# Two chained transformer blocks on one core: attention products gathered into runs, and the recurrence's output products split by shape

## The chip, the cores and the metric

The kernel runs on 1 core of one Trainium2 chip. The metric is the device time of one execution in microseconds, the median of several runs. Engines are called PE (TensorE, matmul), PEld (its weight loads), DVE (VectorE), ACT (ScalarE), POOL (GpSimd) and SP (SyncE, which issues most DMAs). Every time below is in us unless marked ns.

## The reference

512 tokens and 256 context tokens of width 1024 pass through two chained blocks. The first has two layers, an even one (latent attention beside a convolution) and an odd one (a recurrence in two directions beside a neighbourhood attention), each followed by 16 experts; the second has a forgetting attention and a sparse attention, each followed by a convolution FFN. What the change touches, cut short:

```python
def dense_attention(q, k, v):                      # even layer, 8 heads, q/k 96, v 64
    s = jnp.einsum('bqhd,bkhd->bhqk', q, k).astype(jnp.float32) * scale
    return jnp.einsum('bhqk,bkhd->bqhd', jax.nn.softmax(s, -1), v)
# tokens: keys and values of tokens and context (768); context: of the context alone (256)

def wkv7_step(S, inp):                             # odd layer, 8 heads of 64, both directions
    r, w, k, v, a, b = inp
    sa = jnp.einsum('bhvk,bhk->bhv', S, a)
    S = S * w[:, :, None, :] + sa[..., None] * b[:, :, None, :] + v[..., None] * k[:, :, None, :]
    return S, jnp.einsum('bhvk,bhk->bhv', S, r)

# forgetting attention, 16 heads of 64, causal, 512 tokens
s = jnp.einsum('bhqd,bhkd->bhqk', qb, k) * scale + cb[..., :, None] - c[..., None, :]
p = jax.nn.softmax(jnp.where(causal, s, -jnp.inf), axis=-1)
o = jnp.einsum('bhqk,bhkd->bqhd', p, v)

# sparse attention, 16 heads in 2 key groups: compressed, selected and window parts, gated
o = g[:, :, 0] * o_c + g[:, :, 1] * o_s + g[:, :, 2] * o_w
```

## The kernel before

`body` (line 2871) runs the stages one behind the other: `even_stage`, `moe`, `odd_stage`, `moe`, `fa_stage`, `conv_ffn`, `ns_stage`, `conv_ffn`. A scheduler that simulates the engines sets the order of instructions on each engine, except inside `attend` (line 575), which fixes the order on PE and ACT by hand.

**The attentions.** `attend` gives each group of heads two passes. The first pass computes scores with queries on the partitions to find a normaliser per query (its log-sum, turned into the tile `LT`). The second pass computes scores again with keys on the partitions, adds the normaliser as one more matmul (line 542, `S.add`), takes an exponential on ACT into a tile `PT`, and multiplies `PT` with the values. A step of the loop at line 595 issues, in this order: a piece of side work, the first pass's scores of this step, the exponential of the second pass's last step (`b1`), the products of the step before that (`b2`), the second pass's scores of this step, the first pass's exponentials. So the products of a tile stand two steps behind its scores.

- Even attention (`even_attend`, line 1472): `second` walks over the pairs of heads, in a pair over its two heads, in a head over seven key tiles of 128: tiles 0 to 5 for the 512 tokens' queries, and step 6 with the context's queries against the two context tiles. Each step makes one score bank (line 1488, three split products for each), one exponential of 128 × 512 and one product (line 1502; line 1505 in step 6, two of 256 columns). The product's output has 64 rows, so one head fills one half (`HALF`) of a bank's partitions. `PT` has 4 buffers, score banks (`tb`) 2, output banks 2. The conv of the even layer runs on DVE, POOL and ACT beside the first stretch of it.
- Forgetting attention (`fa_attend`, line 779): `second` walks over pairs of heads and four key tiles; a step has both heads of a pair: two score banks, two exponentials (line 805), two products (line 813), which write the two halves of one bank. Tile j has 512 − 128 j columns. `PT` has 6 buffers.
- Sparse attention (`ns_attend`, line 1166): the same with two branches b (selected and window); scores at lines 1186 to 1188, exponential at 1195, products at 1203.

**The recurrence.** `odd_stage` (line 2665) runs `rec_steps` (line 2499) for the context (b = 0) and the two halves of the tokens (b = 1, 2), four chunks of 64 tokens each. `chunk(s)` prepares what doesn't depend on the state; `scan(s)` carries the state S: x = A·S (line 2567, 64 × 64 tiles, 16 matmuls), added on DVE (line 2568); Z·x (line 2572), copied to `UV`; the new state from `UV` and `BT` (line 2580); and for b > 0 the output y: for each of 16 units (8 pairs of head and direction by two heads) S·R (line 2592, 64 × 64 tiles) and `UV`·`AMr` (line 2593, 128 × 64) into the same 64 × 64 piece of one bank, then an add on DVE (line 2600). There are 8 scan steps with y. Banks of the recurrence (`rb`) number 5 (`ODD_BANKS`). Beside it the scheduler weaves the neighbourhood attention (`odd_attend`), the output product of the odd layer (`odd_out`, line 2361) and `ada_steps` (line 1624), which computes the second layer's modulation from 24 loads `aw` of 512 KB through one buffer (line 1644).

## Time and profile before

| | us |
|---|---|
| median of 3 runs | 4043.91 |
| lowest to highest | 4041.24 to 4044.95 |
| the profiled execution | 4059.11 |
| its span | 4057.0 |
| its mean granted TensorE clock | 0.944 |

Where the edited code lies in the span of the profiled execution: even attention, second passes from 366 to 527; the outputs y of the recurrence from 1775 to 2042; products of the forgetting attention from 2790 to 2887; of the sparse attention from 3471 to 3652.

How to read it: the span is one execution from its first instruction to its last. An engine's busy time counts its instructions, not its waits. The granted clock is the share of full speed that PE was given (1.00 is 2.4 GHz, 0.50 is 1.2 GHz). In a timeline neighbouring instructions of the same kind are one entry, with their count behind "x"; starts of successive entries tell how long PE was held, since the end of one overlaps the start of the next. A matmul of fp32 operands counts as two passes in the even and later attentions' products and in the recurrence (so 16 matmuls are x32).

### The profile page before, as it was taken

Reading aid. Unit: us, or ns where it says so; the run is one execution under the profiler, and the core shown is the slowest. Engines: PE = TensorE matmul, PEld = TensorE weight load, DVE = VectorE, ACT = ScalarE, POOL = GpSimd, SP = SyncE. Lnnn points to the kernel's source line nnn. Section 1 sums busy time; section 2 is a strip of 40 time slices with the busy share of each in tenths; the row PEclk is TensorE's granted clock in tenths of the full one; section 3 lists DMA queues with packets and bytes.
Section 4 is the critical chain, followed back from the end, with each engine's and each line's share of the span. In section 5 each row is a group of like instructions: output and inputs, shape, how many; then the busy total and the mean of one; then the engine's idle time right before and its main releaser. Section 6 shows DMA issues by size and latency. Waiting matters only on the chain.

```text
span 4057.0 us, 53307 instructions
## 1 busy us (share of the span) xinstructions
PE 3757.1 (93%) x21365; PEld 2531.7 (62%) x21365; DVE 2090.8 (52%) x3363; ACT 1591.7 (39%) x2687; POOL 493.0 (12%) x603
## 2 busy tenths in 40 slices
PE   7999997999998989798979988899999998999999
PEld 4666474656565778676643332376688876557887
DVE  4747337777777564635252222464355556425544
ACT  3446424555554622431121000257433335643332
POOL 1542011000002122313010000220000012100000
PEclk8998998999998999788879999999999999999999
DMA  7430027888883461214279999622223231003231
GB/s 238 150 117 16 16 103 293 345 317 349 311 338 140 165 189 58 63 33 143 70 282 398 407 411 418 245 89 89 83 95 97 89 95 46 1 27 104 94 99 68
DMA packets 264344, 678.69 MB, mean 167 GB/s; under 512 B 16048, under 2 KB 142016, under 8 KB 214816
## 3 DMA queue, kind: packets, MB, share of 16 engines
q1 hardware_dynamic: 256832, 653.48, 43.9%
q0 software_dynamic: 7264, 21.80, 1.7%
q8 instruction: 168, 2.75, 0.3%
q14 instruction: 80, 0.66, 0.0%
HBM read 641.86 MB, written 32.83 MB: 166 GB/s over the span
## 4 chain that ended last, share of the span: by engine, by line
PE 39%; DMA 12%; DVE 2%; ACT 1%; issue 1%; POOL 0%; SPq 0%; POOLq 0%; ACTq 0%; DVEq 0%
PE bk L374 26%; DMA mw<-in_moe_w_dram 9%; DMA aw<-in_ada_w_dram 1%; PE bk L1992 1%; PE ob L1203 1%; PE rb L2593 1%; PE rb L2592 1%; PE tb L1186 1%; PE bk L1644 1%; PE tb L542 1%; DMA w<-in_a_w_in_dram 1%; PE tb L1187 0%; PE ob L813 0%; PE ob L374 0%; PE bk L2361 0%
## 5 line engine op out<-in xcount | busy, mean ns | idle before, releaser
L351 DVE TENSOR_TENSOR wl<-w,wh 128x1024 fp32r<-128x1024 f32 (+2 forms) x157 | 256.4, 1637 | 280.2 <-ACT wh L350 279.7
L350 ACT CAST wh<-w 128x1024 fp32r<-128x1024 f32 (+2 forms) x157 | 215.6, 1375 | 393.9 <-PE bk L374 341.0
L351 DVE TENSOR_TENSOR wpl<-mw,wph 128x1024 fp32r<-128x1024 f32 x256 | 302.1, 1221 | 31.5 <-ACT wph L350 22.7
L374 PE MATMUL bk<-xTh,wh 128*128 128x512 f32 x704 | 275.7, 393 | 6.9 <-DVE xTl L354 6.9
L350 ACT CAST wph<-mw 128x1024 fp32r<-128x1024 f32 x256 | 258.3, 1047 | 48.7 <-PE bk L1919 30.5
L374 PE MATMUL bk<-xTl,wh 128*128 128x512 f32 x704 | 275.3, 391 | 0.0
L374 PE MATMUL bk<-xTh,wl 128*128 128x512 f32 x704 | 275.3, 391 | 0.0
L1992 PE MATMUL bk<-mw,xgT 128*64 128x512 f32 x1024 | 239.5, 604 | 24.4 <-DMA mw<-in_moe_w_dram 23.5
L2028 PE MATMUL bk<-mw,hidT 128*64 128x512 f32 x1024 | 250.1, 615 | 1.2 <-ACT hidT L2020 0.7
L1992 PEld LDWEIGHTS bk<-mw,xgT 128*64 128x64 f32 x1024 | 70.3, 138 | 177.0 <-issue 129.3
L1919 PE MATMUL bk<-wph,xgPh 128*96 128x512 f32 x512 | 162.3, 397 | 1.3 <-ACT xgPh L1896 1.3
L1919 PE MATMUL bk<-wph,xgPl 128*96 128x512 f32 x512 | 160.2, 394 | 0.0
L1919 PE MATMUL bk<-wpl,xgPh 128*96 128x512 f32 x512 | 158.3, 394 | 0.0
L2028 PEld LDWEIGHTS bk<-mw,hidT 128*64 128x64 f32 x1024 | 72.5, 140 | 136.0 <-issue 126.7
L374 PEld LDWEIGHTS bk<-xTh,wh 128*128 128x128 f32 x704 | 133.4, 190 | 35.2 <-DVE xTl L354 7.3
L374 PEld LDWEIGHTS bk<-xTl,wh 128*128 128x128 f32 x704 | 133.3, 189 | 27.5
L374 PEld LDWEIGHTS bk<-xTh,wl 128*128 128x128 f32 x704 | 133.0, 189 | 27.9
L1877 POOL DMA_INDIRECT xg<-moe_xn,IDX x32 | 31.9, 997 | 878.9 <-PE tb L1889 852.9
L374 PE MATMUL bk<-wh,gTh 128*128 128x512 f32 x352 | 136.9, 389 | 0.0
L374 PE MATMUL bk<-wl,gTh 128*128 128x512 f32 x352 | 136.9, 389 | 0.0
L374 PE MATMUL bk<-wh,gTl 128*128 128x512 f32 x352 | 136.9, 389 | 0.0
L253 POOL TENSOR_TENSOR hr<-hr,mhalf 128x4 f32<-128x4 f32 (+3 forms) x77 | 91.6, 1197 | 262.3 <-DVE hr L485 256.8
(771 smaller groups left out, 8402.4 us busy)
## 6 DMA issues: line engine op xcount, KB each, us to landing
mw<-in_moe_w_dram SPq DMA_DIRECT2D x384, 1024.0 KB, 11.1
aw<-in_ada_w_dram SPq DMA_DIRECT2D x96, 512.0 KB, 4.3
w<-in_f_w_up_dram SPq DMA_DIRECT2D x40, 1024.0 KB, 5.1
w<-in_f_w_down_dram SPq DMA_DIRECT2D x16, 1024.0 KB, 4.9
w<-in_a_w_in_dram SPq DMA_DIRECT2D x24, 512.0 KB, 3.5
w<-in_od_w_in_dram SPq DMA_DIRECT2D x15, 512.0 KB, 4.5
w<-in_ev_w_in_dram SPq DMA_DIRECT2D x12, 512.0 KB, 4.8
rw_bk<-bk SPq DMA_DIRECT2D x8, 768.0 KB, 4.2
```

Source lines behind the costliest of these rows:

```text
L253: return self.nc.gpsimd.tensor_tensor(t, t, self.mhalf[:p].to_broadcast([p, n]), op=ALU.pow)
L350: nc.scalar.copy(h, src)
L351: nc.vector.tensor_sub(l, src, h.bitcast(F32))
L374: self.nc.tensor.matmul(out, lhsT=L[a], rhs=R[b], start=start and n == 0, stop=stop and n == len(pairs) - 1)
L542: self.k.nc.tensor.matmul(s, lhsT=self.k.selb[0:self.nr, h:h + 1].to_broadcast([self.nr, 128]), rhs=LT, start=False, stop=stop)
L1186: nc.tensor.matmul(s[:, q0:], lhsT=KA[:, b, kv, sl], rhs=QA[:, h, q0:], start=True, stop=False)
L1203: nc.tensor.matmul(o[HALF[u], q0:], lhsT=V[j][:, b, kv * 64:(kv + 1) * 64], rhs=PT[u][:, q0:], start=b == 0 and j == 0, stop=False)
L1644: nc.tensor.matmul(ps[32 * g:32 * g + 32, :], lhsT=k.silc[:, kk, :], rhs=w[:, kk - k0, :], start=kk < 4, stop=kk >= 4)
L1919: at = nc.tensor.matmul(ps[hf], lhsT=t[a][:, kk, :], rhs=parts[b][:, kk % MOE_WK, hf * 512:hf * 512 + 512], start=kk + n == 0, stop=kk + n ...
L1992: nc.tensor.matmul(ps[64 * hf:64 * hf + 64, :], lhsT=t[:, kk, :], rhs=w[kk // 2][:, kk % 2, hf * 512:hf * 512 + 512], start=kk == 0, stop= ...
L2028: at = nc.tensor.matmul(px[64 * dh:64 * dh + 64, :], lhsT=hTx(q, c), rhs=w2[q][:, c, dh * 512:dh * 512 + 512], start=q + c == 0, stop=q + ...
L2592: nc.tensor.matmul(y[r, col(u)], lhsT=S[r, u, :], rhs=G.R[r, s // 2, d, ct, hd, t], start=True, stop=False)
```

## The change

In the even attention the two heads of a pair go together: the loop is now over key tiles and in each over the two heads, `products` gathers exponential tiles in `ready`, and after both heads of tiles 1, 3, 5 it issues the four products of two tiles, after tile 6 the four of the context; the exponential tiles number 8 instead of 4. In the forgetting and the sparse attention `products` gathers likewise, and on every second key tile issues four (two tiles, two heads); `PT` goes from 6 buffers to 8. In the recurrence the 16 S·R products are issued together, right behind x and ahead of Z, into the bank of y, which is opened there; the 16 products with `AMr` stay where y was and add to it. Nothing is added or taken away in the number of matmuls, exponentials or loads.

```diff
@@ -637,6 +637,7 @@
 
 
 PUTS = 3
+AT_PT = 8
 NORM_POOL = 1, 4
 
 
@@ -784,7 +785,7 @@
 
     def second(g, LT):
         for p in g:
-            ob = []
+            ob, ready = [], []
             for j in range(4):
                 q0 = j * 128
                 sl = slice(q0, q0 + 128)
@@ -801,16 +802,22 @@
 
                 def exps(p=p, j=j, q0=q0, ST=ST, PT=PT):
                     for u in range(2):
-                        t = Q.tile([128, 512], F32, name="PT", tag="PT", bufs=6)
+                        t = Q.tile([128, 512], F32, name="PT", tag="PT", bufs=AT_PT)
                         nc.scalar.activation(t[:, q0:], ST[u][:, q0:], AF.Exp, scale=-1.0, bias=ncT[:, j, 2 * p + u:2 * p + u + 1])
                         PT.append(t)
 
-                def products(p=p, j=j, q0=q0, PT=PT, ob=ob):
+                def products(p=p, j=j, PT=PT, ob=ob, ready=ready):
+
                     if j == 0:
                         ob.append(k.obank())
-                    for u in range(2):
-                        h = 2 * p + u
-                        nc.tensor.matmul(ob[0][HALF[u], q0:], lhsT=V[j][:, h * 64:(h + 1) * 64], rhs=PT[u][:, q0:], start=j == 0, stop=j == 3)
+                    ready.append((j, PT))
+                    if j % 2 == 0:
+                        return
+                    for jj, ts in ready:
+                        for u, t in enumerate(ts):
+                            h, qs = 2 * p + u, slice(128 * jj, 512)
+                            nc.tensor.matmul(ob[0][HALF[u], qs], lhsT=V[jj][:, h * 64:(h + 1) * 64], rhs=t[:, qs], start=jj == 0, stop=jj == 3)
+                    ready.clear()
                     if j == 3:
                         split_copy(nc, oh[:, p, :], ol[:, p, :], ob[0])
                 yield scores, exps, products
@@ -1173,7 +1180,7 @@
     def second(g, LT):
         for p in g:
             kv = p // 4
-            ob = []
+            ob, ready = [], []
             for b in range(2):
                 for j in range(4):
                     q0 = j * 128
@@ -1191,17 +1198,22 @@
 
                     def exps(q0=q0, ST=ST, PT=PT):
                         for u in range(2):
-                            t = Q.tile([128, 512], F32, name="PT", tag="PT", bufs=6)
+                            t = Q.tile([128, 512], F32, name="PT", tag="PT", bufs=AT_PT)
                             nc.scalar.activation(t[:, q0:], ST[u][:, q0:], AF.Exp, scale=-1.0)
                             PT.append(t)
 
-                    def products(p=p, kv=kv, b=b, j=j, q0=q0, PT=PT, ob=ob):
+                    def products(p=p, kv=kv, b=b, j=j, PT=PT, ob=ob, ready=ready):
                         if b == 0 and j == 0:
                             ob.append(k.obank())
                         o = ob[0]
-                        for u in range(2):
-                            nc.tensor.matmul(o[HALF[u], q0:], lhsT=V[j][:, b, kv * 64:(kv + 1) * 64], rhs=PT[u][:, q0:],
-                                             start=b == 0 and j == 0, stop=False)
+                        ready.append((j, PT))
+                        if j % 2 == 0:
+                            return
+                        for jj, ts in ready:
+                            for u, t in enumerate(ts):
+                                nc.tensor.matmul(o[HALF[u], 128 * jj:], lhsT=V[jj][:, b, kv * 64:(kv + 1) * 64], rhs=t[:, 128 * jj:],
+                                                 start=b == 0 and jj == 0, stop=False)
+                        ready.clear()
                         if b == 1 and j == 3:
                             for u in range(2):
                                 c0 = 32 * ((2 * p + u) % 4)
@@ -1474,10 +1486,10 @@
     nc = k.nc
 
     def second(g, LT):
-        ob = []
-        for h in (2 * g, 2 * g + 1):
-            r = HALF[h % 2]
-            for j in range(7):
+
+        ob, ready = [], []
+        for j in range(7):
+            for h in (2 * g, 2 * g + 1):
                 ST, PT = [], []
 
                 def scores(h=h, j=j, ST=ST):
@@ -1490,20 +1502,26 @@
                     ST.append(s)
 
                 def exps(ST=ST, PT=PT):
-                    t = P.tile([128, 512], F32, name="PT", tag="PT", bufs=4)
+                    t = P.tile([128, 512], F32, name="PT", tag="PT", bufs=EV_PT)
                     nc.scalar.activation(t, ST[0], AF.Exp, scale=-1.0)
                     PT.append(t)
 
-                def products(h=h, j=j, r=r, PT=PT, ob=ob, g=g):
+                def products(h=h, j=j, PT=PT, ob=ob, ready=ready, g=g):
                     if not ob:
                         ob.extend((k.bank(), k.bank()))
-                    v = slice(h * 64, (h + 1) * 64)
-                    if j < 6:
-                        nc.tensor.matmul(ob[0][r, :], lhsT=E.V[j][:, v], rhs=PT[0], start=j == 0, stop=j == 5)
-                    else:
-                        for u in range(2):
-                            nc.tensor.matmul(ob[1][r, 0:256], lhsT=E.V[4 + u][:, v], rhs=PT[0][:, 256 * u:256 * u + 256], start=u == 0, stop=u == 1)
-                    if h % 2 and j >= 5:
+                    ready.append((j, h, PT[0]))
+                    if h % 2 == 0 or j in (0, 2, 4):
+                        return
+                    for jj, hh, t in ready:
+                        r, v = HALF[hh % 2], slice(hh * 64, (hh + 1) * 64)
+                        if jj < 6:
+                            nc.tensor.matmul(ob[0][r, :], lhsT=E.V[jj][:, v], rhs=t, start=jj == 0, stop=jj == 5)
+                    for u in range(2 if j == 6 else 0):
+                        for _, hh, t in ready:
+                            nc.tensor.matmul(ob[1][HALF[hh % 2], 0:256], lhsT=E.V[4 + u][:, hh * 64:(hh + 1) * 64],
+                                             rhs=t[:, 256 * u:256 * u + 256], start=u == 0, stop=u == 1)
+                    ready.clear()
+                    if j >= 5:
                         o, t = (ob[0], slice(0, 512)) if j == 5 else (ob[1][:, 0:256], slice(512, 768))
                         split_copy(nc, KA[:, 2 * g, 0, t], KA[:, 2 * g, 1, t], o)
                         E.done += j == 6
@@ -1615,6 +1633,7 @@
 
 
 EV_NORM = 1, 3, 5
+EV_PT = 8
 EV_ADA = 12, 1024
 EV_HEADS, EV_BANKS = (14, 2), (2, 2, 2)
 EV_MODS, EV_PAUSE, EV_W, EV_POOL = 0.7, 2, (3, 2), (2,)
@@ -2567,6 +2586,11 @@
                 nc.tensor.matmul(x[r, col(u)], lhsT=A[r, s // 2, d, ct, hd, t], rhs=S[r, u, :], start=True, stop=True)
             nc.vector.tensor_add(xs, v8(x), xs)
         yield ROOM[4]
+        if b:
+
+            y = k.rbank()
+            for u, d, ct, hd, r in units:
+                nc.tensor.matmul(y[r, col(u)], lhsT=S[r, u, :], rhs=G.R[r, s // 2, d, ct, hd, t], start=u == 0, stop=False)
         ps = [k.rbank(), k.rbank()]
         for ct, d, hd in pairs:
             nc.tensor.matmul(ps[hd][HALF[d], col(ct)], lhsT=Z[HALF[hd], 8 * s + 4 * d + ct, :], rhs=xs[HALF[hd], 4 * d + ct, :], start=True, stop=True)
@@ -2587,10 +2611,8 @@
                 nc.vector.tensor_mul(G.S, G.S, wb)
             yield ROOM[4]
         if b:
-            y = k.rbank()
             for u, d, ct, hd, r in units:
-                nc.tensor.matmul(y[r, col(u)], lhsT=S[r, u, :], rhs=G.R[r, s // 2, d, ct, hd, t], start=True, stop=False)
-                nc.tensor.matmul(y[r, col(u)], lhsT=UV[:, u, hd, :], rhs=R["AMr"][:, d, ct, hd, :], start=False, stop=True)
+                nc.tensor.matmul(y[r, col(u)], lhsT=UV[:, u, hd, :], rhs=R["AMr"][:, d, ct, hd, :], start=False, stop=u == 7)
             for d in range(2):
                 t0 = 256 * b - 256 + 64 * s
                 t0 = 448 - t0 if d else t0
```

How the order of PE moves. In the even attention, a stretch without a first pass, before (line 1488 scores, 542 the normaliser, 1502 a product; `V_389` is the values of a key tile):

```order
L1502 MATMUL bk<-PT,V_389 64x512
L1488 MATMUL tb<-QA,KA 128x512 x3
L542 LDWEIGHTS selb
L542 MATMUL tb<-LT,selb 128x512
L1502 MATMUL bk<-PT,V_390 64x512
```

The same stretch in the changed kernel, where the lines are 1500, 542 and 1518:

```order
L1500 MATMUL tb<-QA,KA 128x512 x3
L542 LDWEIGHTS selb
L542 MATMUL tb<-LT,selb 128x512
L1500 MATMUL tb<-QA,KA 128x512 x3
L542 LDWEIGHTS selb
L542 MATMUL tb<-LT,selb 128x512
L1518 MATMUL bk<-PT,V_391 64x512 x2
L1518 MATMUL bk<-PT,V_392 64x512 x2
```

A product stood between every two scores; now four stand together, and up to three steps of scores follow one another.

The last scan step of the recurrence on PE, before:

```order
L2554 MATMUL rb<-q_15823,AMk 64x64 x16
L2567 MATMUL rb<-S,A 64x64 x16
L2572 MATMUL rb<-x,Z 64x64 x16
L2592 MATMUL rb<-R,S 64x64
L2593 MATMUL rb<-AMr,q_15823 64x64
L2592 MATMUL rb<-R,S 64x64
L2593 MATMUL rb<-AMr,q_15823 64x64
```

and in the changed kernel (x is line 2586, S·R 2593, Z 2596, the products with `AMr` 2615):

```order
L2573 MATMUL rb<-q_15823,AMk 64x64 x16
L2586 MATMUL rb<-S,A 64x64 x16
L2593 MATMUL rb<-R,S 64x64 x16
L2596 MATMUL rb<-x,Z 64x64 x16
L2615 MATMUL rb<-AMr,q_15823 64x64 x16
L2664 MATMUL bk<-y,c_rw 128x512 x4
```

The 16 alternations became a run of 16 ahead of Z and a run of 16 behind it. In the other scan steps the scheduler still puts other work of the stage inside these runs.

In the sparse attention, ahead of a product, before (line 1154 to 1156 the first pass, 1203 products, 1186 and 1187 scores):

```order
L1155 MATMUL bk<-KL,QA 128x128
L1156 LDWEIGHTS identb
L1156 MATMUL bk<-causalb,identb 128x128
L1203 MATMUL ob<-PT,V_23541 64x384 x2
L1186 MATMUL tb<-QA,KA 128x128
L1187 MATMUL tb<-QA,KL 128x128
```

and in the changed kernel:

```order
L1162 MATMUL bk<-KL,QA 128x128
L1163 LDWEIGHTS identb
L1163 MATMUL bk<-causalb,identb 128x128
L1214 MATMUL ob<-PT,V_23540 64x512 x2
L1214 MATMUL ob<-PT,V_23541 64x384 x2
L1193 MATMUL tb<-QA,KA 128x128
L1194 MATMUL tb<-QA,KL 128x128
```

The products of two key tiles stand in a row; the step before has none.

## Rows read from the trace of the kernel before

**Rows 1.** Stretches: us, busy (x instructions) of each engine, granted clock, DMA share, GB/s
```profile
366.00:425.00 59.00, 55.66 (x205) 31.44 (x206) 44.50 (x60) 27.75 (x59) 0.00 (x0) 0.88 0.00 1
425.00:527.00 102.00, 99.62 (x328) 42.82 (x326) 16.68 (x35) 41.50 (x71) 0.00 (x0) 0.98 0.05 16
1775.00:2042.00 267.00, 246.20 (x2805) 178.09 (x2801) 96.83 (x192) 50.10 (x106) 46.02 (x61) 0.84 0.32 98
2790.00:2822.00 32.00, 29.71 (x196) 18.24 (x195) 12.23 (x50) 28.34 (x75) 0.00 (x0) 1.00 0.18 53
3513.00:3580.00 67.00, 65.50 (x415) 38.75 (x416) 25.83 (x57) 45.51 (x142) 0.00 (x0) 1.00 0.00 1
```

**Rows 2.** The chain of waits in 1770 to 2045, by line
```profile
by line: DMA aw<-in_ada_w_dram 17.9%; PE rb L2593 13.4%; PE rb L2592 13.3%; PE bk L1644 9.6%; PE bk L2361 5.9%; PE rb L2528 4.6%; PE rb L2548 4.1%; issue 2.8%; PE bk L1658 2.1%; PE rb L2580 1.7%; PE bk L1652 1.3%; PE rb L2537 1.3%; DMA b__1
```

**Rows 3.** Timeline of PE, even attention: start us, us, engine line op out<-in
```profile
489.73 0.39 PE L542 MATMUL tb<-LT,selb 96*128 96x512 bf16 x1
490.05 1.07 PE L1502 MATMUL bk<-PT,V 128*64 128x512 f32 x2
491.05 0.97 PE L1488 MATMUL tb<-QA,KA 96*128 96x512 f32 x3
...
496.25 0.28 PE L542 MATMUL tb<-LT,selb 96*128 96x256 bf16 x1
496.46 1.07 PE L1502 MATMUL bk<-PT,V 128*64 128x512 f32 x2
```

**Rows 4.** Timeline of PE, forgetting attention
```profile
2802.32 1.08 PE L813 MATMUL ob<-PT,V 128*64 128x512 f32 x4
...
2810.47 0.44 PE L813 MATMUL ob<-PT,V 128*64 128x128 f32 x4
...
2826.49 0.45 PE L796 MATMUL tb<-QA,KA 128*128 128x384 f32 x1 [0.48 <-ACT PT L805]
```

**Rows 5.** Timeline of PE, two y steps of the recurrence
```profile
1806.97 0.33 PE L2592 MATMUL rb<-R,S 64*64 64x64 f32 x2
1807.22 0.33 PE L2593 MATMUL rb<-AMr,q 128*64 128x64 f32 x2
...
2041.79 0.47 PE L2592 MATMUL rb<-R,S 64*64 64x64 f32 x2
2042.20 0.47 PE L2593 MATMUL rb<-AMr,q 128*64 128x64 f32 x2
```

**Rows 6.** Timeline of PE, runs in one shape
```profile
1795.82 1.10 PE L2567 MATMUL rb<-S,A 64*64 64x64 f32 x32
...
1860.90 1.15 PE L2580 MATMUL rb<-q,q 128*64 128x64 f32 x32
```

**Rows 7.** PE's lines in 1775 to 2042: x | busy us, mean ns | idle before
```profile
L2593 PE MATMUL rb<-AMr,q 128*64 128x64 f32 x254 | 50.4, 291 | 0.8 <-DVE q L2575 0.8
L2592 PE MATMUL rb<-R,S 64*64 64x64 f32 x256 | 49.9, 285 | 0.0
L1644 PE MATMUL bk<-aw,silc 128*32 128x512 f32 x96 | 29.9, 706 | 16.5 <-DMA aw<-in_ada_w_dram 16.5
...
L2580 PE MATMUL rb<-q,q 128*64 128x64 f32 x192 | 8.1, 225 | 0.0
...
L2567 PE MATMUL rb<-S,A 64*64 64x64 f32 x224 | 7.8, 218 | 0.0
```

**Rows 8.** Timeline of PE, products of the aw loads
```profile
1980.80 1.05 PE L1644 MATMUL bk<-aw,silc 128*32 128x512 f32 x4 [0.86 <-DMA aw<-in_ada_w_dram]
...
1995.55 1.92 PE L1644 MATMUL bk<-aw,silc 128*32 128x512 f32 x4
...
2000.97 1.05 PE L1644 MATMUL bk<-aw,silc 128*32 128x512 f32 x4
...
2010.45 1.05 PE L1644 MATMUL bk<-aw,silc 128*32 128x512 f32 x4
```

**Rows 9.** DVE's lines in 1775 to 2042
```profile
L2568 DVE TENSOR_TENSOR x<-rb,x 128x512 f32<-128x512 f32 x7 | 4.8, 687 | 9.0 <-PE rb L2567 9.0
```

## The prediction

> **What bounds the kernel now.** TensorE (PE) does nearly all of the work of this kernel, so the question in each edited stretch is whether PE or a wait for another engine ends last there. I read the busy times by stretch first, which answer that [rows 1]. In the second part of the even attention (425–527 us) PE is busy 99.6 of 102 us and the vector engine (DVE) 16.7: PE is the bound. In its first part (366–425) PE has 55.7 of 59, but DVE has 44.5, so there is little room under it. The recurrence (1775–2042) has PE at 246.2 of 267 and a granted clock of 0.84. In the forgetting attention (2790–2822) PE has 29.7 of 32 with the scalar engine (ACT) at 28.3: nearly two bounds. In the sparse attention (3513–3580) PE has 65.5 of 67, ACT 45.5.
>
> The chain of waits for 1770–2045, grouped by line, then says what sets the end of the recurrence [rows 2]: lines 2592 and 2593, which form y, hold 13.3% and 13.4% of 275 us, that is 73 us; loads of `aw` hold 17.9%.
>
> **Even attention.** A step of the second pass alone is in [rows 3]: the correction of the scores at 489.73, the product of one head at 490.05, the next scores at 491.05. So the product has 1.00 to its exit. To enter it costs some 0.11: from the correction's start to the product's it is 0.32 with 512 columns and 0.21 with 256 (496.25 to 496.46), so 256 columns are 0.107, and 0.32 less two of them is the entry. One head's product fills one half of the array's columns. How two heads' products do side by side is in [rows 4], where the forgetting attention issues both: the four passes last 1.08, the two of one head in [rows 3] 1.07. So two heads cost what one costs. Four with 128 columns last 0.44: 384 columns more for 0.64, or 1.67 ns a column, so 512 columns are 0.853, and of the 1.00 some 0.15 is the exit. Into a run of products and out again is 0.26.
>
> Before, 56 steps (4 pairs of heads, 2 heads, 7 tiles) cost 1.11 each: 62.2 us. Now each pair of heads has three runs of two tiles (2 × 0.853 + 0.26 = 1.97) and one of the context's tile (1.11): 4 × 7.02 = 28.1. That removes 34.1, or 0.61 a step. In the second part 42 of the steps lie; 25.5 go, less 2.7 which I allow for the waits on DVE and ACT as heads' norms come in: 22.8. In the first part 14 steps lie, worth 8.5, but DVE's 44.5 of 59 us come in bursts from the conv; I take half, 4.2. Even attention: **27** (from 17, two thirds of the 25.5 and nothing in the first part, to 34). The eight exponential tiles cost nothing on an engine; they let ACT run ahead while products are gathered.
>
> **Recurrence.** Before, S·R (line 2592, 64 × 64 tiles) and the product with AMr (line 2593, 128 × 64) alternate 16 times in each of 8 scan steps. Each starts 0.25 us after the last at the full clock, 0.41 at the lower one [rows 5]. In one shape the same passes run far closer: line 2567, which has exactly S·R's shape, does 32 passes in 1.10 us, and line 2580, with the shape of the other, 32 in 1.15 [rows 6]. A matmul here is two passes, so 16 of each shape are 2.3 us in runs and 8.2 alternating. Averaged over the stretch, clock dips included, 7 runs of line 2567 cost 7.8 us and 6 of line 2580 8.1 [rows 7]: 1.11 + 1.35 = 2.46 a step, 19.7 for 8. I take these away from the chain's 73: **54**.
>
> The upper end: the two lines' busy time is 49.9 + 50.4 = 100.3 us [rows 7], in which each entry of 0.33 overlaps the next by 0.08 (of 0.47 by 0.06); without the overlaps 77 to 87. 87 − 19.7 = 67. The lower end is where the loads pace the stretch. Each `aw` load waits for its one buffer; with a y step between two uses they lie 14.75 apart (1980.80 to 1995.55), without one 5.4 (1995.55 to 2000.97) [rows 8]. Two y steps lie so between loads (18.7); two lie at or behind the last load's product at 2010.45, each worth 73/8 − 2.46 = 6.7 (13.5); one more shares its interval with other work, for which I count 6; three lie ahead of the first load and count nothing. Together 38.
>
> What the edit adds: the bank of y is one of the five of the recurrence, and it is now held from ahead of Z until the add on DVE. If that blocked a bank once per step, PE would wait for an eviction, near the 0.69 us of a DVE add of this size [rows 9]: 8 × 0.7 = 5.5 us, inside the lower end. S·R on the other hand stands where PE waits for the add behind x, and fills it. What is behind the recurrence on the path (the second experts' loads start when its space comes free) shifts with it one to one.
>
> **A rule that speaks against the run of S·R.** Line 2567 puts two diagonal 64 × 64 tiles, with different rows, into one bank, and does 32 passes in 1.10 us, so 34 ns a pass; a 64-column pass alone would be 64 × 1.67/2 = 53 ns, so the two overlap [rows 4, 6]. The Trainium skill (TensorEngine Tiling (Array Packing), Gotcha 1: PSUM Pressure) states that different row tiles cannot access the same PSUM bank at the same time. By that rule a run of S·R into y's one bank would take 1.7 instead of 1.1, an estimate from that page, and the odd stage would gain 8 × 0.6 = 4.8 us less, 3961; the trace speaks against it, and the sum does not use it.
>
> **Later attentions.** Products of two tiles in a row halve the entries: in the forgetting attention 32 groups become 16, 16 × 0.26 = 4.2; in the sparse one 64 become 32, 8.3. Against it: on the steps without products PE reaches the next scores sooner and they need a score bank that ACT has yet to read. The row at 2826.49 shows it today, 0.48 us of waiting for line 805 [rows 4]. At worst every second step pays that: 16 × 0.48 = 7.7 and 32 × 0.48 = 15.4. ACT is nearer the bound in the first. I take 2 and 5 (ends −3.5 to 4.2, −7.1 to 8.3): **7**.
>
> **Sum.** 27 + 54 + 7 = 88 us off the profiled execution, 4059.1 with a span of 4057.0, which gives 3971; the profiled one lies 15 us over the median of 4043.9. Taken off the median: **3956**. With all terms at their upper ends, 34 + 67 + 13 = 114, 3930; at the lower, 17 + 38 − 3 = 52, 3992 (both attentions at their worst together I leave out).
>
> **The rivals.** *A: the loads keep the recurrence's pace.* The 17.9% of the chain on `aw` speak for it, the fact that PE waits only 16.5 us for these loads against it [rows 7]. Then 38 instead of 54: 3972. *B: the steps without products wait* for ACT in the last two attentions, giving −10 instead of 7: 3973. For it, ACT's 28.3 of 32; against it, 45.5 of 67 and two more exponential tiles. *C: the change doesn't do what it says in the even attention*: the heads of a pair don't overlap, and only the entries fall, 56 to 16: 40 × 0.26 = 10 in place of 27, 3973. Against it stand the four passes in 1.08 us of [rows 4], from the same shapes. *D, on the other side: the clock.* Within a y step the spacing goes from 0.25 to 0.41 [rows 5], so the granted clock does fall in this stretch. Suppose the compact runs, with their waits in between, leave it at the lower level from 1775 on: 246.2 busy at 0.84 are 207 us of full-clock work, of which the 256 entries at 0.25 (64) shrink to 17, leaving 160; at 0.5 that is 320, and with 21 us idle 341 instead of 267: 74 lost, less 34 won elsewhere, 4084. It decides from a mean granted clock of 0.57 down, where 160/0.57 + 21 is 34 over 267. Against it: the clock of 0.84 now goes with the passes that fill the array least, and those are what is removed. The Trainium skill (TensorE: Matmul & The Clock Gate, What's actually happening) states that the throttled state is the default and that activity releases it; by that rule, denser runs should raise the clock and D is the less likely; the rows agree as far as they go, since the clock falls inside the y steps and not in line 2567's run.
>
> **How the numbers follow.** Forecast 0.64; A 0.14; B 0.10; C 0.05; D 0.03; a loss elsewhere that eats the gain 0.04. A, B and C all end inside 3930 to 3992, so that range holds over 8 in 10 with what the forecast's own case leaves at its edges. A change under 0.2% (8 us) is about what a measurement of this kernel cannot tell from none. Faster by more: 0.94; within: 0.02; slower: 0.04 (D and a part of the last).
>
> **What would show each step.** Even: runs of four products of some 1.9 us with no gap, and the attention ending some 27 us sooner than the 161 it takes; if it gained 10, C is right or DVE has taken over, which DVE's idle time tells. Recurrence: runs of 16 S·R and 16 AMr products of 1.0 to 1.4 us; the chain of 1770 to its end without those lines, the `aw` products near 5 us apart if A is right, and a granted clock near or above 0.84 (below 0.57 would be D). Later attentions: products in runs of four with 0.26 saved per pair of tiles, against waits on ACT ahead of scores. Wrong would be the prediction as a whole if the 73 us of the chain turned out to be cover for something that is late anyway.

## The result, and the profile after

The changed kernel takes 3946.35 us, median of 4 runs (3941.87 to 3952.56), against 4044.43 for the kernel before; the ratio is 0.9759, with a 95% interval of 0.9742 to 0.9776, so 98 us less (91 to 104). A second measurement of the same two kernels, in five rounds, gave 0.9739 (0.9714 to 0.9765). The profiled execution took 3948.89, with a span of 3947.1, 110 us under the span of before; 12 of the 110 are that the profiled execution of before lay well above its median.

The page of the changed kernel, its span and part 1 (busy us, share of the span):

```profile
span 3947.1 us, 53296 instructions
...
PE 3625.0 (92%) x21365; PEld 2471.7 (63%) x21365; DVE 2090.8 (53%) x3363; ACT 1588.8 (40%) x2687; POOL 491.6 (12%) x603
```

The same stretches as [rows 1], moved to where they lie now (us, busy time of PE, PEld, DVE, ACT, POOL, granted clock, DMA share, GB/s):

```profile
366.00:420.00 54.00, 50.50 (x206) 32.50 (x206) 43.08 (x58) 27.73 (x59) 0.00 (x0) 0.81 0.00 1
420.00:503.00 83.00, 79.94 (x328) 43.39 (x329) 18.11 (x37) 42.03 (x72) 0.00 (x0) 0.90 0.06 19
1731.00:1941.00 210.00, 185.03 (x2961) 139.15 (x2959) 107.49 (x207) 56.08 (x121) 49.02 (x63) 0.93 0.40 120
2694.00:2725.00 31.00, 28.21 (x199) 18.45 (x198) 12.51 (x53) 28.07 (x74) 0.00 (x0) 1.00 0.16 53
3410.00:3470.00 60.00, 59.86 (x408) 37.72 (x406) 22.99 (x48) 41.66 (x133) 0.00 (x0) 1.00 0.00 1
```

The two parts of the even attention's second passes are 54 and 83 us instead of 59 and 102; the stretch with y is 210 instead of 267, its PE busy 185 instead of 246, at a granted clock of 0.93 instead of 0.84. PE is busy for 88% to 100% of each stretch and remains the bound.

The chain of waits around the recurrence, by line, which answers to [rows 2]:

```profile
by line: DMA aw<-in_ada_w_dram 29.4%; PE bk L1663 11.5%; PE bk L2380 10.8%; PE bk L2342 4.9%; PE rb L2547 4.2%; DMA c_rw<-in_consts_dram 3.5%; PE bk L1677 3.5%; PE rb L2567 3.2%; PE rb L2604 2.3%; PE rb L2593 2.2%; PE bk L2355 2.2%; PE rb L
```

The lines that form y, with 26.7% the largest holder before, are down to 2.2% for S·R (now line 2593); the loads of `aw` lead with 29.4%.

Where the time went, stage by stage, from the first and last starts of PE's lines at the stages' borders (us, in the profiled execution of each kernel; by the lines of before: "even" from line 1459 to 1784, "odd" from 2162 to 2642, the group norm behind the recurrence; "FA" and "NS" the forgetting and the sparse attention):

| kernel | even | odd | second experts, FA's input | FA | first FFN | NS |
|---|---|---|---|---|---|---|
| before | 298.8 | 711.5 | 732.3 | 108.4 | 579.4 | 188.4 |
| after | 273.6 | 639.4 | 733.7 | 106.0 | 574.5 | 182.1 |
| even edit alone | 268.1 | 717.8 | 736.1 | 107.9 | 575.9 | 188.5 |
| heads joined, no pairs of tiles | 270.0 | 708.2 | 723.6 | 107.4 | 575.7 | 188.5 |
| recurrence's edit alone | 295.7 | 644.8 | 731.0 | 107.8 | 575.9 | 190.0 |
| later attentions alone | 297.8 | 711.3 | 729.4 | 105.7 | 571.3 | 182.2 |
| lagged y | 297.5 | 687.9 | 732.3 | 108.6 | 575.0 | 188.5 |
| runs of y at the old place | 298.5 | 654.2 | 732.5 | 108.1 | 578.9 | 190.1 |

The first column runs from the even attention's first scores to the experts' router, so other work of the even layer is in it, and its differences are what counts. Each row is one execution. A second execution of the changed kernel has 273.7, 637.3, 732.1, 105.5, 578.7 and 182.2, so one kernel differs by 2 us in the odd stage and 4 in the FFN. Between all the traces, stages that no edit touches differ by more (the second experts from 717 to 736, the FFN from 571 to 579).

What PE does in the odd stage, from the same traces. "Held" is the time from an instruction's start to the next start, less the engine's wait; a line's busy time counts the overlaps too. The matmuls are the same in all columns, only their order differs (us):

| odd stage | before | lagged y | runs of y at the old place | recurrence's edit alone | all edits |
|---|---|---|---|---|---|
| held by the two lines of y | 81.2 | 57.1 | 18.2 | 17.1 | 16.7 |
| held by all other matmuls | 567.3 | 567.4 | 563.7 | 556.9 | 542.8 |
| PE idle (its waits) | 63.1 | 63.4 | 72.3 | 70.8 | 79.9 |
| granted clock | 0.88 | 0.89 | 0.90 | 0.91 | 0.93 |

### The profile page after: what moved, and what is told of

Its sections match the earlier page's. It is cut to its first block, busy times and chain, and to the rows that moved or that the text cites. A ratio compares the mean times of both kernels' runs of the same rounds, so it can differ in the third digit from the quotient of the medians.

```text
span 3947.1 us, 53296 instructions
## 1 busy us (share of the span) xinstructions
PE 3625.0 (92%) x21365; PEld 2471.7 (63%) x21365; DVE 2090.8 (53%) x3363; ACT 1588.8 (40%) x2687; POOL 491.6 (12%) x603
## 4 chain that ended last, share of the span: by engine, by line
PE 47%; DMA 12%; DVE 4%; ACT 2%; issue 1%; POOL 1%; SPq 0%; POOLq 0%; DVEq 0%; ACTq 0%
PE bk L374 31%; DMA mw<-in_moe_w_dram 9%; DMA aw<-in_ada_w_dram 2%; PE bk L2011 2%; PE ob L1214 1%; PE bk L2342 1%; PE tb L1193 1%; PE bk L1663 1%; PE bk L2380 1%; PE tb L542 1%; DVE wl L351 1%; PE tb L1194 0%; PE ob L374 0%; DMA w<-in_a_w_in_dram 0%; PE rb L2547 0%
## 5 line engine op out<-in xcount | busy, mean ns | idle before, releaser
L2011 PE MATMUL bk<-mw,xgT 128*64 128x512 f32 x1024 | 238.7, 602 | 26.7 <-DMA mw<-in_moe_w_dram 25.8
```

The lines of the kernel that those rows point to most:

```text
L2011: nc.tensor.matmul(ps[64 * hf:64 * hf + 64, :], lhsT=t[:, kk, :], rhs=w[kk // 2][:, kk % 2, hf * 512:hf * 512 + 512], start=kk == 0, stop= ...
```

## The experiments

**The three edits, each alone.** Each keeps the kernel before and takes one part of the change: the even attention with its eight exponential tiles; the recurrence; the forgetting and sparse attention with theirs.

```diff
+        for j in range(7):
+            for h in (2 * g, 2 * g + 1):
...
+EV_PT = 8
```

> The edit of the even attention alone, everything else as before. In the two traces the second passes of the even attention end 25 us sooner. If these 25 us are this edit's and the later stages only shift with it: 25 us off, ratio 0.994. Rival: the trace's stages are one execution each, and the profiled execution of before was 15 us over its median; if part of the 25 is that, 15 us or less, ratio 0.996 or above.

Measured: ratio 0.9935 (0.9919 to 0.9951), 26 us (20 to 33).

```diff
+            y = k.rbank()
+            for u, d, ct, hd, r in units:
+                nc.tensor.matmul(y[r, col(u)], lhsT=S[r, u, :], rhs=G.R[r, s // 2, d, ct, hd, t], start=u == 0, stop=False)
         ps = [k.rbank(), k.rbank()]
```

> The edit of the recurrence alone. Theory: the odd stage lost 72 us between the two traces, because passes of two shapes in turn are slow and seven of the eight scan steps pass this on in full; some 60 to 72 us off, ratio 0.982 to 0.985. Rival, the prediction's own sum by the chain: 54 us, ratio 0.987. Rival, the loads pace the stage: 38 us, ratio 0.991.

Measured: ratio 0.9865 (0.9846 to 0.9884), 55 us (47 to 62).

```diff
+AT_PT = 8
...
+                    ready.append((j, PT))
+                    if j % 2 == 0:
+                        return
```

> The edits of the forgetting and the sparse attention alone, with their eight exponential tiles. From the two traces 2 us in the first and 7 in the second: 9 us off, ratio 0.998. Rival: the steps without products wait for ACT and give it all back: ratio 1.000.

Measured: ratio 0.9960 (0.9945 to 0.9975), 16 us (10 to 22).

0.9935 × 0.9865 × 0.9960 = 0.9762, against 0.9759 for all: the parts add up within their intervals, so no part is seen to live on another. The timed runs give the recurrence the chain's 54 and not the 72 of the two traces; both are weighed below.

**What makes y slow.** The product with AMr of a unit is issued four units behind its S·R, so shapes still take turns, but no product adds at once to the piece written just ahead of it:

```diff
-            for u, d, ct, hd, r in units:
-                nc.tensor.matmul(y[r, col(u)], lhsT=S[r, u, :], rhs=G.R[r, s // 2, d, ct, hd, t], start=True, stop=False)
-                nc.tensor.matmul(y[r, col(u)], lhsT=UV[:, u, hd, :], rhs=R["AMr"][:, d, ct, hd, :], start=False, stop=True)
+            for i in range(16 + 4):
+                if i < 16:
+                    u, d, ct, hd, r = units[i]
+                    nc.tensor.matmul(y[r, col(u)], lhsT=S[r, u, :], rhs=G.R[r, s // 2, d, ct, hd, t], start=u == 0, stop=False)
+                if i >= 4:
+                    u, d, ct, hd, r = units[i - 4]
+                    nc.tensor.matmul(y[r, col(u)], lhsT=UV[:, u, hd, :], rhs=R["AMr"][:, d, ct, hd, :], start=False, stop=u == 7)
```

> The kernel before, with the product with AMr of a unit issued four units behind its S·R: shapes still take turns (24 of the former 31 changes stay between single matmuls of unlike shape, at the old place), but no product adds at once to the piece that the one ahead of it has just written. If the turn of shapes costs the 0.25 us: ratio 0.995 to 1.000, spacing 0.25. Rival, the wait is for the sum in the same piece of the bank: spacing near 0.07 us, and most of the gain of the recurrence's edit, ratio 0.985 to 0.990.

Measured: ratio 0.9941 (0.9922 to 0.9961), 24 us (16 to 32): a little more than the first theory gave, far less than the second. The timeline of PE in one y step says why (start us, us, line, tile, passes):

```profile
2007.01 0.33 PE L2594 MATMUL rb<-R,S 64*64 64x64 f32 x2
2007.27 0.33 PE L2597 MATMUL rb<-AMr,q 128*64 128x64 f32 x2
2007.52 0.33 PE L2594 MATMUL rb<-R,S 64*64 64x64 f32 x2
2007.78 0.33 PE L2597 MATMUL rb<-AMr,q 128*64 128x64 f32 x2
```

The spacing of the single matmuls is 0.25 to 0.26, as in [rows 5], though the two neighbours now write different pieces. So the sum in one piece is not the cause; the turn of shapes is. The gain is that of the products now out of the turns: in each step five S·R and five products with AMr stand in runs, and 23 of the 31 changes of shape are left (the expectation has 24). The lines of y hold PE 57.1 us instead of 81.2, 24 less, while the rest of the stage and the waits stay as they were; the expectation left this out of its ratio.

**The place of S·R.** Both runs stand where y was, behind the new state:

```diff
             for u, d, ct, hd, r in units:
-                nc.tensor.matmul(y[r, col(u)], lhsT=S[r, u, :], rhs=G.R[r, s // 2, d, ct, hd, t], start=True, stop=False)
-                nc.tensor.matmul(y[r, col(u)], lhsT=UV[:, u, hd, :], rhs=R["AMr"][:, d, ct, hd, :], start=False, stop=True)
+                nc.tensor.matmul(y[r, col(u)], lhsT=S[r, u, :], rhs=G.R[r, s // 2, d, ct, hd, t], start=u == 0, stop=False)
+            for u, d, ct, hd, r in units:
+                nc.tensor.matmul(y[r, col(u)], lhsT=UV[:, u, hd, :], rhs=R["AMr"][:, d, ct, hd, :], start=False, stop=u == 7)
```

> The kernel before, with the 16 S·R in a run and then the 16 products with AMr in a run, both at the old place behind the new state, and y's bank opened there. If the gain of the recurrence's edit is the end of the turns of shape alone, this gives what the edit alone gave (ratio 0.9865, within 0.002). Rival: the place counts too, since S·R ahead of Z fills the wait for DVE's add behind x; that wait was 0.87 us in one step of the lagged kernel, so 8 x 0.9 = 7 us less, ratio 0.9883.

Measured: ratio 0.9864 (0.9838 to 0.9891), the same as with S·R ahead of Z. In one step of it the two runs are

```profile
1809.46 1.15 PE L2592 MATMUL rb<-R,S 64*64 64x64 f32 x32
1810.54 1.15 PE L2594 MATMUL rb<-AMr,q 128*64 128x64 f32 x32
```

each 32 passes in 1.08 and 0.98 from start to start. The place is worth nothing that the timed runs can tell; in the traces the odd stage is 9 us longer with the old place (654.2 against 644.8), and which of the two holds is not settled.

**What carries the even gain.** Both heads together, but their products as soon as both are there, for every key tile (shown against the even edit):

```diff
-if h % 2 == 0 or j in (0, 2, 4):
+if h % 2 == 0:
     return
```

> The even edit alone, but products issued for every key tile as soon as both heads are there (28 runs of two products instead of 16, all with 8 exponential tiles). By the prediction's working two heads side by side carry nearly all: 12 more entries at 0.26 are 3 us less than the even edit's 26, ratio 0.9943. Rival: the length of the runs carries it, half of the gain or less, ratio 0.9965 or above.

Measured: ratio 0.9915 (0.9894 to 0.9936), 34 us; more than the 26 with runs of two tiles, though the intervals overlap. In the table the even stage is 2 us longer this way (270.0 against 268.1), as two heads side by side with more entries should be; the 3 us less that were expected hold there and not in the total. The rest is behind it: with the runs of two tiles the odd stage takes 717.8 and the second experts 736.1, this way 708.2 and 723.6. Nothing in either stage is edited; but the odd stage's order on PE, the same entries, agrees in the traces with that of before to 99% here and to some 80% with the runs of two tiles. The scheduler laid the odd stage out anew. That the other order is what costs some 10 us is argued from one trace of each, not shown; on top of the whole change it came out the other way (637.3 and 639.4 with runs of two tiles, 645.5 without).

**The loads of the modulation.** In the changed kernel the `aw` products late in the recurrence lie 5 us apart, with short waits for the load (the column in brackets):

```profile
1885.74 1.05 PE L1663 MATMUL bk<-aw,silc 128*32 128x512 f32 x4 [0.66 <-DMA aw<-in_ada_w_dram]
...
1890.74 1.05 PE L1663 MATMUL bk<-aw,silc 128*32 128x512 f32 x4
...
1895.70 1.05 PE L1663 MATMUL bk<-aw,silc 128*32 128x512 f32 x4 [0.80 <-DMA aw<-in_ada_w_dram]
...
1900.63 1.05 PE L1663 MATMUL bk<-aw,silc 128*32 128x512 f32 x4 [0.62 <-DMA aw<-in_ada_w_dram]
```

> The changed kernel, with only the first of the four loads of each modulation piece made in the odd layer; the products of the other three use the same tile, so that the modulation of the second layer is not the reference's. Loads of 512 KB in the odd stage fall from 24 to 6. In the changed kernel PE waits 22 us for these loads, the last eleven of them 5 us apart. If they pace the end of the recurrence now: 15 to 25 us under the changed kernel, ratio to before 0.970 to 0.972. Rival: the recurrence's own dependencies would hold PE at these places anyway: ratio 0.975 to 0.977.

```diff
-                w = P.tile([128, kn, 512], F32, name="aw", tag="aw", bufs=nslot)
-                k.load = nc.sync.dma_start(w, k.wsrc(W)(k0, kn, c0, 512))
+                if k0 == 0 or i == 0:
+                    w = P.tile([128, kn, 512], F32, name="aw", tag="aw", bufs=nslot)
+                    k.load = nc.sync.dma_start(w, k.wsrc(W)(k0, kn, c0, 512))
```

Measured: ratio 0.9624 (0.9599 to 0.9648), well under both expectations: about 50 us less than the changed kernel; in the traces the odd stage falls from 639.4 to 608.7. Most of what is left lies in the even stage (6 less) and the second experts (7 less), which this doesn't edit.

> The kernel before, with 6 instead of 24 loads of 512 KB in the odd layer's modulation, the products using the same tile (so the modulation is not the reference's). The changed kernel gained 53 us by this. If the loads became the pace only with the edit, since the y steps gave them time before: a third of that or less here, 0 to 18 us, ratio 0.9955 or above. Rival, the loads cost the same on both sides: 50 us, ratio 0.988.

The same edit as the last, in the kernel before. Measured: ratio 0.9919 (0.9889 to 0.9949), 33 us (21 to 45); the odd stage falls from 711.5 to 677.8. So in the odd stage this edit gives 34 us before and 31 after. The theory that the loads became the pace only with the change falls: in this stage they cost about the same on both sides, and the gain of the recurrence came beside them. In the timed totals neither number was forecast: 33 lies above the 18 of the one expectation and under the 50 of the other.

Not all of it is waiting. In the changed kernel the `aw` products hold PE 26.9 us and wait 22.3; with a quarter of the loads 16.9 and 1.2, together 31 less, the whole of the stage's gain. Before, 28.4 and 16.5 became 16.8 and 3.0, 25 of the 34. The products hold PE for less because those of one tile no longer wait for a load each and stand in runs of up to eight.

> The changed kernel, with the modulation's loads of the odd layer in halves (48 of 256 KB) through two buffers of half the size, so the same space. If the wait for the one buffer is the pace: most of the 22 us that PE waits go, ratio to before 0.971 to 0.973. Rival: a load in halves brings its bytes no faster, and two in flight share what one had: ratio 0.976.

```diff
-ODD_AW = 1, 1024
+ODD_AW = 2, 512
```

Measured: ratio 0.9725 (0.9701 to 0.9748). PE's waits for these loads, of the changed kernel and then with halves (us in total, times, longest):

```profile
PE bk L1663 <- DMA aw<-in_ada_w_dram: 22.2, 15, 4.1
```

```profile
PE bk L1663 <- DMA aw<-in_ada_w_dram: 5.7, 5, 2.2
```

Most of the wait is gone, as meant, and yet the odd stage is 646.4 us, 7 more than without. The products themselves took it back. With halves each load brings one product (x2) instead of two (x4):

```profile
1900.74 1.04 PE L1663 MATMUL bk<-aw,silc 128*32 128x512 f32 x2
1901.71 0.44 PE L2567 MATMUL rb<-R,BK 128*64 128x128 f32 x4
1902.35 1.05 PE L1663 MATMUL bk<-aw,silc 128*32 128x512 f32 x2
1903.33 0.62 PE L2573 MATMUL rb<-q,AMk 64*64 64x64 f32 x25
```

A product of 32 columns' width alone holds PE 0.98, as long as two in a row in the rows above, where the second writes another quarter of the bank's partitions. Over the stage the `aw` products hold PE 50.6 us instead of 26.9: 24 more, against 17 less of waiting, which is the 7. The lower total lies in the second experts (723.6 against 733.7) and the even stage (268.1 against 273.6), which the edit doesn't touch.

**Versions on top of the change.** The joined heads and the halves were tried together with the change, beside the change again.

> The changed kernel, with the even products issued for every key tile (both heads together, no two tiles in a row). In the traces the even stage itself is 2 us longer so. If the difference between the two even edits alone (26 and 34 us) came from the order of the odd stage, which the scheduler lays out anew for each, there is no rule in it: the changed kernel's own time within 8 us, ratio to before 0.974 to 0.978. Rival: runs of two tiles cost more than they give in any kernel: 6 to 10 us under the changed kernel, ratio 0.9735 or less.

The edit of the joined heads above, in the changed kernel. Measured: 0.9723 (0.9694 to 0.9751).

> The same with the modulation's loads of the odd layer in halves through two buffers. If the halves take away the pace of the loads whatever the order: 10 to 14 us under the kernel without halves, ratio 0.971 to 0.973. Rival: the gain of the halves was the order's too: ratio 0.976.

That and `ODD_AW = 2, 512`. Measured: 0.9764 (0.9739 to 0.9789).

> The changed kernel itself, beside the three others on the same chip: ratio 0.976, within 0.002.

Measured: 0.9739 (0.9714 to 0.9765), at the lower edge of what was expected.

Products for every tile come out 11 us under the change beside them (3931.13 against 3942.41), which is the rival's number, but with intervals that overlap: not a version shown to be better. Halves, which seemed worth 6 to 14 us with the one order, cost 20 with the other; the odd stage again is 7 us longer with them (652.5 against 645.5), and again the `aw` products hold PE for longer (50.8 against 26.1) than the wait gets shorter (5.3 against 22.7). Nothing of the halves' gain carries over.

## Why the prediction was right, point by point

The forecast was 3956, the result 3946; the range of 3930 to 3992 held it. The rise was to come as 27 + 54 + 7; the edits alone measured 26 + 55 + 16. The first term came out by its mechanism; that the second came out is in part luck, as told below; the third was too small by the timed runs, and near the 8.7 of the traces.

**Even attention: right, 27 against 26.** The mechanism is in this timeline of PE (start us, us, line, tile):

```profile
443.76 1.25 PE L1500 MATMUL tb<-QA,KA 96*128 96x512 f32 x3
444.85 0.39 PE L542 MATMUL tb<-LT,selb 96*128 96x512 bf16 x1
445.17 1.94 PE L1518 MATMUL bk<-PT,V 128*64 128x512 f32 x8
447.03 0.96 PE L1500 MATMUL tb<-QA,KA 96*128 96x512 f32 x3
```

Eight passes, two tiles of two heads, take 1.86 from start to start, after an entry of 0.32 − 0.21 = 0.11: with both 1.97, which is the sum's figure to the hundredth. Nine of the twelve runs take this; the other three take 2.4 to 3.6, the two longest of them at a granted clock of 0.60 and 0.50. Rival C (the heads of a pair don't overlap) falls, since four products of one head each, at 1.00, would have taken 4. What the sum didn't have is the clock: the second part was granted 0.90 in this execution, against 0.98 in [rows 1], and with the same edit alone 1.00:

```profile
420.00:497.00 77.00, 72.82 (x331) 39.36 (x330) 16.62 (x36) 42.52 (x74) 0.00 (x0) 1.00 0.06 20
```

In that execution the even stage is 5.5 us shorter. So the edit's own worth in the stage is 25 to 31 us by trace, and the clock goes with where in it.

**What lies behind an edit shifts with it one to one: true behind the recurrence, not behind the even attention.** The prediction says it of the second experts, and with the recurrence's edit alone they take 731.0 where they took 732.3. For the even attention the sum takes the same without saying so, and **there this step failed**, though it didn't show in the total: in the traces the even edit alone brings 31 us in its stage and loses 6 of them in the odd stage, which is laid out in another order. A scheduler that times the whole program passes on more than a shift.

**Recurrence: the mechanism right, its size open between two readings.** The last scan step of the changed kernel:

```profile
1935.72 1.10 PE L2586 MATMUL rb<-S,A 64*64 64x64 f32 x32
1936.65 1.10 PE L2593 MATMUL rb<-R,S 64*64 64x64 f32 x32
1937.69 0.69 PE L2596 MATMUL rb<-x,Z 64*64 64x64 f32 x32
1939.23 1.15 PE L2615 MATMUL rb<-AMr,q 128*64 128x64 f32 x32 [0.85 <-DVE q L2599]
1946.82 1.19 PE L2664 MATMUL bk<-y,c_rw 128*128 128x512 f32 x1 [6.43 <-DMA c_rw<-in_consts_dram]
```

S·R takes 1.04 to the next start and the products with AMr 1.15, where the 16 alternations took 8 to 13. By lines in 1731 to 1941 (x | busy us, mean ns | idle before):

```profile
L1663 PE MATMUL bk<-aw,silc 128*32 128x512 f32 x96 | 28.3, 671 | 22.3 <-DMA aw<-in_ada_w_dram 22.2
...
L2593 PE MATMUL rb<-R,S 64*64 64x64 f32 x256 | 10.3, 222 | 0.0
L2615 PE MATMUL rb<-AMr,q 128*64 128x64 f32 x256 | 10.1, 223 | 0.9 <-DVE q L2599 0.9
```

10.3 + 10.1 = 20.4 us for the eight steps; the sum had 19.7. What was taken away was to be the chain's 73. Timed alone, the edit gives 55 (47 to 62), where 73 − 19.7 gives 54. The traces give 67 for the odd stage with this edit alone and 72 with all, at or over the sum's upper end. By what PE does there (the second table), y's two lines go from 81.2 us held to 17.1 with this edit alone, 64 less; the working of the upper end, 77 to 87 less 19.7, was nearer to this than the chain's 73. Two things that the sum didn't have then nearly cancel: the other matmuls hold PE 10 us less at a higher granted clock, and its waits grow by 8. With all edits these are 25 and 17. So that 54 met 55 is in part luck.

The clock shows in windows at the end: before, the last 52 us ahead of the group norm, and six of them within a y step:

```profile
1992.00:2044.00 52.00, 48.12 (x526) 33.81 (x526) 10.55 (x20) 6.20 (x14) 1.83 (x4) 0.73 0.26 85
2036.00:2042.00 6.00, 6.00 (x32) 4.24 (x31) 0.00 (x0) 0.00 (x0) 0.00 (x0) 0.50 0.06 23
```

and the last 50 of the changed kernel:

```profile
1895.00:1945.00 50.00, 39.24 (x814) 28.89 (x814) 16.67 (x32) 10.45 (x23) 2.10 (x4) 0.98 0.37 117
```

Before, the clock fell to its lower level within seven of the eight y steps (they were granted 0.61 to 0.80; the first, 1.00) and stood at 0.73 over the stretch; now it stands at 0.98, with half again as many matmuls in 50 us as before in 52. The sum left the clock of the other work as it was: that is the term which was too small by the traces. Why the timed runs give less than the traces is only in part told. The profiled execution of the edit alone was the lowest of its four, 6 us under their median, and if these 6 lay in this stage, 67 would be 61, inside the timed interval. That of before was above its median, but hardly here: with the later attentions alone, in an execution 2.5 us above its median, the odd stage takes 711.3 too. What is left of the difference stays open.

**Rival A (the loads keep the pace)** fell in its own form. PE's waits for `aw` grew from 16.5 to 22.3 us and the last loads stand 5 us apart, as A had it; yet the edit gave 55 timed and 67 to 72 in the traces, not 38, and in this stage the loads cost about as much before as after. The price of 38 counted the three steps ahead of the first load at nothing; between the Z products of successive steps, the changed kernel took 10.0, 10.9 and 8.8 us less there, 0.4 only in the one interval that the loads fill (from 1850 to 1946 before), 7.5, 12.3 and 12.6 in the next three, and 5.9 from the last Z to the group norm.

**Rival D (the clock)** went the other way: up, not down, from 0.84 to 0.93 in the stretch. The Trainium skill (TensorE: Matmul & The Clock Gate, What's actually happening) says that the throttled state is the default and that activity releases it. The rise agrees with this as far as it goes, but PE was busy for 92% of the stretch before and for 88% of it after, so the rule alone doesn't tell the two kernels apart.

A run of 16 S·R, whose neighbours lie in different row halves, took 1.04 into one bank in this kernel. The Trainium skill (TensorEngine Tiling (Array Packing), Gotcha 1: PSUM Pressure) says that different row tiles can't use one PSUM bank at the same time. By that rule the prediction estimated 1.7 for the run; the measurement decides against it here.

**Later attentions: 7 forecast, 8.7 in the stages' own times (2.4 and 6.3), 16 (10 to 22) timed.** In the forgetting attention runs of four products stand as meant, and the step behind reaches its scores early:

```profile
2695.24 1.72 PE L819 MATMUL ob<-PT,V 128*64 128x512 f32 x8
2696.89 0.33 PE L797 MATMUL tb<-QA,KA 128*128 128x128 f32 x1
...
2699.83 0.50 PE L797 MATMUL tb<-QA,KA 128*128 128x512 f32 x1 [1.30 <-ACT PT L806]
```

The first row's 1.65 for eight passes is the run; the last shows 1.30 of waiting for ACT's exponential (line 806), which the sum had at 0.48 a time. Over the whole attention these waits are, before and after (us, times, longest):

```profile
PE tb L796 <- ACT PT L805: 1.5, 3, 0.6
```

```profile
PE tb L797 <- ACT PT L806: 2.2, 5, 1.3
```

So B, with 0.48 on every second step, fell: five waits in sixteen, 0.7 us more in all. In the sparse attention PE waits once for its exponential on either side, 1.5 us before and 1.2 after. The 7 us between 9 and 16 I can't place; the FFN, which no edit touches, differs by that between the traces.

**A new wait, not foreseen:** behind the last y, PE waits 6.43 us for the constants of the group norm (`c_rw`), 1.9 before. The recurrence ends sooner than this load.

## What to carry to other kernels

Matmuls that take turns between two tile shapes can cost several times their columns: look for pairs of lines that alternate in the timeline at one spacing whatever their size, and issue each shape in a run, into one bank if need be. Products that each fill a part of the array's columns belong next to each other: two heads with half of them each here, and two `aw` products with a quarter each, where loads so small that the products come singly cost more than the wait that they removed. More tiles in a row add little. Where a scheduler orders the whole program by its own clock, an edit in one stage reorders the next, so measure each edit alone before a few us are put down to it.

## What the runs showed of the hardware

A product of 64 × 64 and one of 128 × 64 in turn start 0.25 us apart at a granted clock of 1.00 and 0.40 at 0.50, whether or not the second adds to what the first wrote; in runs of one shape the same products are 0.06 to 0.07 us apart. What in the turn costs this, no run tells. The clock fell within the turns: six us inside one y step were granted 0.50, and with y in runs at its old place all eight y steps were granted 1.00. One fp32 product of 128 × 32 with 512 columns holds PE 0.98 us, two in different column quarters side by side the same, eight in a row 1.85. Taking away three quarters of the odd stage's loads shortened that stage by 31 to 34 us on either side, of which PE's waits for them were 14 to 21; a buffer that removed most of the waits, but parted the products, lengthened it by 7.
